# Attention on one core: twelve of 31 head pairs transpose their queries and keys by DMA, and VectorE takes a seventh group of exponentials

## The chip, the cores and the metric

One core of one Trainium2 chip. The metric is device microseconds of that core, as the median of several executions. The profiled span is about 1.8 us shorter than the time of the same execution, so spans are compared only with spans.

Short names: SP is the sync engine, on whose instruction queue nearly all transfers are issued one after the other; PE is TensorE, ACT is ScalarE, DVE is VectorE, POOL is GpSimd. A *pair* is two heads of one batch, a *group* is two score blocks of 128 x 512 that one exponential takes. A pair has four groups.

## The reference

```python
# q, k, v: (8, 8, 512, 64) float32
scale = 1.0 / np.sqrt(q.shape[-1])
scores = np.einsum('bhqd,bhkd->bhqk', q, k) * scale
scores = scores - scores.max(axis=-1, keepdims=True)
attn = np.exp(scores)
attn = attn / attn.sum(axis=-1, keepdims=True)
return np.einsum('bhqk,bhkd->bhqd', attn, v).astype(np.float32)
```

## The kernel before

It walks through 32 pairs. For each: load q, k and v (256 KB each); cast q and k on POOL to fp16 with the two heads side by side (`qkp`); transpose them, eight 128 x 128 transposes on PE into PSUM and one DVE copy back (`tqk`); scores on PE; exponentials on ACT; values on PE with a column of ones for the sum; normalise on DVE; store from SP. Six of the groups have their exponential computed on DVE, in seven passes each. A planner (`Plan`) models the engines with constants in nanoseconds and fixes the order of the instructions.

```python
class Plan:
    SLOT, EXP, EXP_DONE, EXP_FIXED = 216, 853, 1085, 51
    COPY, NORM, NORM_COLUMN = 700, 380, 67
    RAISE, PASSES, LATE = 1216, (867, 822, 1400, 1400, 1400, 1372), 700
    # ... cut
    def for_dve(self, m):                    # may group m go to DVE?
        g = self.groups[m][0][0]
        return (m > 5 and g < self.pairs - 3 and not self.passes
                and not any(x[1] == "raise" for x in self.ready))

    def scores(self, t):
        # ... cut: every fourth group is preceded by a "feed" of its pair
        if m % 4 == 0 and grp[0][0] > 0 and len(grp) == 2:
            self.note(t, "feed", grp[0][0])
# ... cut
    lpool = ctx.enter_context(tc.tile_pool(name="load", bufs=6))
    qpool = ctx.enter_context(tc.tile_pool(name="qk16", bufs=3))
    tpool = ctx.enter_context(tc.tile_pool(name="tqk", bufs=4))

    def feed(g):
        load(g + 5, "kqv")                   # three loads on SP
        cast_qk(g + 3)                       # POOL
        cast_v(g + 2)                        # POOL

    def transposes(g, n, bank):              # half a pair: four on PE
        # ... cut
        for i in range(NI):
            nc.tensor.transpose(tps[g][:, n, i, :], qkp[g][:, n, i, :], ident)

    def copy(g):                             # DVE, PSUM to SBUF
        # ... cut
        nc.vector.tensor_copy(
            out=tqk[g][:, :, :], in_=tps.pop(g).rearrange("p n i c -> p n (i c)"))

    def normalise(u, n):
        # ... cut: reciprocal and multiply on DVE
        while heads and heads[0][2] + NI <= u + n:
            g, h, u0 = heads.pop(0)
            nc.sync.dma_start(               # one store of 128 KB per head, on SP
                out=source(out, g)[:, h], in_=ring[:, u0 % NU : u0 % NU + NI, :])
```

The softmax here doesn't subtract the row's maximum and nothing guards it: scores larger than these inputs give would overflow.

## Time and profile before

| | before |
|---|---|
| time, median of 4 runs | 123.3 us (123.15 to 123.48) |
| profiled span | 121.7 us |
| first exponential begins, last one ends | 5.21 and 117.83 us |
| time lost by ACT between them, added up from the trace | 0.58 us |
| from the last exponential to the end | 3.92 us |
| SP between 20 and 100 us: issuing, waiting | 58.8 us, 13.3 us |

The row for SP is added up from the trace: the durations of its issues, and the pauses of over 0.15 us between them. The exponentials run without a gap and end every 0.918 us; everything else follows them. *Lost* time of ACT means here, and in all that follows, the sum of what the steps from one exponential's end to the next exceed 0.918 us. The time in which no exponential runs at all is less (0.34 us here), because after a pause one takes its full length of some 1.05 us from start to end. Two more lines of before are needed. First from its list of waits (who waited for whom: us in total, times, longest):

```profile
POOL qkp L331 <- DMA k<-in_k_dram: 18.1, 16, 2.9
```

Then the issue of a set of loads in the timeline of SP (start, length, engine, line, operation). Most issues take 0.4 to 0.5 us:

```profile
41.28 0.47 SPq L318 DMA_DIRECT2D k<-in_k_dram  x1
41.79 0.47 SPq L318 DMA_DIRECT2D q<-in_q_dram  x1
42.35 0.42 SPq L318 DMA_DIRECT2D v<-in_v_dram  x1
```

### The profile page before, as it was taken

How to read it: one execution, taken by the hardware profiler on the slowest of the kernel's cores; microseconds unless marked ns; L12 is line 12 of the kernel's file. 1: busy time of each engine (PE TensorE's matmuls, PEld its weight loads, DVE VectorE, ACT ScalarE, POOL GpSimd, SP SyncE). 2: the span in 40 equal slices, each digit the busy share in tenths (PEclk: the TensorE clock that was granted, in tenths of full speed). 3: DMA queues.
4: the chain of work that ended last, by engine and by line, in shares of the span. 5: the costliest groups of instructions: out<-in, count | busy, mean ns of one | idle time of the engine just before them, and what ended most of it. 6: DMA issues, size and time to landing. Idle time of an engine off the chain costs nothing.

```text
span 121.7 us, 3951 instructions
## 1 busy us (share of the span) xinstructions
PE 108.1 (89%) x1557; PEld 67.6 (56%) x1557; DVE 98.5 (81%) x171; ACT 114.4 (94%) x127; POOL 73.9 (61%) x101
## 2 busy tenths in 40 slices
PE   7979788889899798998998998889999998999970
PEld 2556455547466465664565564556655655556550
DVE  1456899989989898699999998986979899876451
ACT  4599999999999999999999999999999999999970
POOL 2368969998487977396587577366794377300000
PEclk9999999999999999999999999999999999999995
DMA  3899999999999989998899967899979995113234
GB/s 117 273 363 384 385 376 384 387 275 282 370 374 352 311 284 318 335 347 276 238 312 297 318 226 251 268 348 343 325 239 281 348 330 196 64 52 126 93 110 152
DMA packets 35603, 33.82 MB, mean 278 GB/s; under 512 B 2688, under 2 KB 35584, under 8 KB 35584
## 3 DMA queue, kind: packets, MB, share of 16 engines
q1 hardware_dynamic: 35152, 33.24, 83.1%
q10 hardware_dynamic: 432, 0.33, 0.9%
q8 instruction: 12, 0.20, 0.7%
q14 instruction: 7, 0.06, 0.2%
HBM read 25.17 MB, written 8.39 MB: 276 GB/s over the span
## 4 chain that ended last, share of the span: by engine, by line
ACT 54%; PE 22%; issue 19%; DVE 2%; ACTq 0%
ACT pt L379 54%; PE st L374 8%; PE o L462 6%; PE st_0a L510 3%; PE tp L348 2%; PE st L553 1%; DVE tqk L353 1%; PE o_last L477 1%; DVE ring L441 1%; PE tp_qb L548 0%; DVE qt L590 0%; DVE obl L490 0%; PE tp_qa L548 0%; PE st_0a L553 0%; DVE rc L440 0%
## 5 line engine op out<-in xcount | busy, mean ns | idle before, releaser
L379 ACT ACTIVATE pt<-st 128x1024 f16<-128x1024 f32 (+1 forms) x120 | 109.4, 1327 | 0.1
L374 PE MATMUL st<-tqk 64*128 64x512 f16 x248 | 48.1, 384 | 7.4 <-ACT pt L379 6.5
L462 PE MATMUL o<-vp,pt 128*128 128x65 f16 x1008 | 46.9, 195 | 1.7 <-ACT pt L379 1.3
L462 PEld LDWEIGHTS <-pt 128*128 128x128 f16 x1008 | 37.0, 98 | 18.8 <-issue 15.0
L331 POOL CAST qkp<-k 128x512 f16<-128x512 f32 x31 | 25.3, 815 | 24.2 <-DMA k<-in_k_dram 18.1
L323 POOL CAST vp<-v 128x512 f16<-128x512 f32 x32 | 27.4, 859 | 1.0 <-DMA v<-in_v_dram 0.9
L374 PEld LDWEIGHTS <-tqk 64*128 64x128 f16 x248 | 13.3, 93 | 20.7 <-issue 12.7
L331 POOL CAST qkp<-q 128x512 f16<-128x512 f32 x30 | 22.7, 756 | 2.4 <-DMA q<-in_q_dram 2.3
L441 DVE TENSOR_TENSOR ring<-o,rc 128x448 f32<-128x448 f32 (+2 forms) x37 | 22.6, 611 | 1.3
L355 DVE COPY tqk<-tp 128x1024 f16<-128x1024 f16 x30 | 20.5, 685 | 3.1 <-PE tp L348 2.8
L348 PE MATMUL tp<-ident,qkp 128*128 128x128 f16 x248 | 19.5, 220 | 0.0
L348 PEld LDWEIGHTS <-qkp 128*128 128x128 f16 x248 | 14.0, 98 | 6.9 <-issue 4.7
L428 DVE SCALAR_TENSOR_TENSOR y<-y,m 128x1024 f32<-128x1024 f32 x12 | 15.9, 1321 | 0.0
L440 DVE RECIPROCAL rc<-o 128x7 f32<-128x7 f32 (+2 forms) x37 | 7.3, 198 | 9.3 <-PE o L462 9.1
L393 DVE TENSOR_SCALAR z<-st 128x1024 uint32<-128x1024 f32 x6 | 7.3, 1221 | 1.1 <-PE st L374 1.1
L428 DVE SCALAR_TENSOR_TENSOR y<-m 128x1024 f32<-128x1024 f32 x6 | 8.2, 1361 | 0.0
L428 DVE SCALAR_TENSOR_TENSOR pt<-y,e 128x1024 f16<-128x1024 f32 x6 | 7.7, 1279 | 0.0
L417 DVE TENSOR_SCALAR e<-z 128x1024 uint32<-128x1024 uint32 x6 | 6.1, 1024 | 0.0
L406 DVE TENSOR_SCALAR m<-z 128x1024 uint32<-128x1024 uint32 x6 | 4.6, 765 | 0.0
L510 PE MATMUL st_0a<-const-bfloat16-1.0 128*128 128x512 bf16 (+1 forms) x11 | 3.5, 482 | 0.8 <-PEq L644 0.8
L510 PEld LDWEIGHTS <-const-bfloat16-1.0 128*128 128x128 bf16 x15 | 1.9, 143 | 2.4 <-issue 2.4
L526 ACT ACT_TABLE_LOAD x1 | 1.3, 1283 | 1.7 <-PEq L644 1.7
(43 smaller groups left out, 18.6 us busy)
## 6 DMA issues: line engine op xcount, KB each, us to landing
out_dram<-ring SPq DMA_DIRECT2D x63, 128.0 KB, 3.8
k<-in_k_dram SPq DMA_DIRECT2D x31, 256.0 KB, 4.8
q<-in_q_dram SPq DMA_DIRECT2D x31, 256.0 KB, 4.9
v<-in_v_dram SPq DMA_DIRECT2D x27, 256.0 KB, 5.3
v<-in_v_dram SPq DMA_DIRECT2D x10, 128.0 KB, 4.4
k<-in_k_dram ACTq DMA_DIRECT2D x2, 128.0 KB, 2.9
q<-in_q_dram SPq DMA_DIRECT2D x2, 128.0 KB, 2.6
out_dram<-obl SPq DMA_DIRECT2D x1, 64.0 KB, 1.8
```

Of the source, the lines that this page charges most:

```text
L323: nc.gpsimd.tensor_copy(out=vps[g % NV][:, :, :, 0:D], in_=raw[g]["v"][:, :, :, :])
L331: eng.tensor_copy(out=t[:, n].rearrange("p i (h d) -> p h i d", h=2), in_=raw[g][name][:, :, :, :],)
L348: nc.tensor.transpose(tps[g][:, n, i, :], qkp[g][:, n, i, :], ident)
L355: nc.vector.tensor_copy(out=tqk[g][:, :, :], in_=tps.pop(g).rearrange("p n i c -> p n (i c)"))
L374: nc.tensor.matmul(st[:, x, :], kc, qc, start=True, stop=True)
L379: nc.scalar.activation(out=pt[:, 0:size, :], in_=st[:, 0:size, :], func=EXP, scale=scale)
L393: nc.vector.tensor_scalar(out=r["z"][:, :, :], in0=r["st"][:, :, :], scalar1=scale * 1.4426950408889634 * 2.0**23, scalar2=(127 + SHIFT) * ...
L428: nc.vector.scalar_tensor_tensor(out=r["pt"][:, :, :] if n == 3 else r["y"][:, :, :], in0=mant if n == 0 else r["y"][:, :, :], scalar=QUAR ...
L440: nc.vector.reciprocal(out=rc[:, 0:n], in_=o[:, x : x + n, D : D + 1])
L441: nc.vector.tensor_tensor(out=ring[:, u % NU : u % NU + n, :], in0=o[:, x : x + n, 0:D], in1=rc[:, 0:n].broadcast_to([P, n, D]), op=AluOp. ...
L462: nc.tensor.matmul(os[u // 7][:, u % 7, :], blocks[(g, c, h)][:, y * P : (y + 1) * P], vps[g % NV][:, h, c, :], start=(c == 0), stop=(c == ...
L510: nc.tensor.matmul(dst[:, 0:n], ones[:, 0:P], ones[:, 0:n], start=True, stop=True)
```

## The change

The intent: exponentials on ACT set the time, and DVE can compute one more group instead if it is spared other work. So pairs 6, 8, ..., 28 get their transposed q and k through a DMA transpose from SBUF to SBUF. That saves 12 copies on DVE and 96 transposes on PE. (v is also loaded in halves for one pair instead of five, `HALVED`: four issues fewer on SP.) It is issued on SP for the pair two ahead, in front of the loads for five pairs ahead. The model's constants are new, the rule for DVE groups allows a seventh, and the last pair does head 0 first, then head 1.

```diff
-    SLOT, EXP, EXP_DONE, EXP_FIXED = 216, 853, 1085, 51
+    SLOT, EXP, EXP_DONE, EXP_FIXED = 216, 853, 181, 64
 ...  (further constants of the model)
+    BY_DMA = (6, 8, 10, 12, 14, 16, 18, 20, 22, 24, 26, 28)
+    LAST_PAIRS, AHEAD, MARGIN, SLACK, MOST = 2, 1, 1.05, 800, 7
-        self.tq = {0: 5800}
+        self.tq = {0: 5800, **{g: 0 for g in self.BY_DMA}}
 ...
-            and g < self.pairs - 3
-            and not self.passes
+            and g < self.pairs - self.LAST_PAIRS
+            and len(self.passes) <= self.AHEAD
+            and len(self.on_dve) < self.MOST
 ...  (order of the last pair; bookkeeping of DVE's model)
+        while self.part_t == 0 and self.next_t in self.BY_DMA:
+            self.next_t += 1
 ...
-    tpool = ctx.enter_context(tc.tile_pool(name="tqk", bufs=4))
+    tpool = ctx.enter_context(tc.tile_pool(name="tqk", bufs=5))
-    HALVED = range(20, 25)
+    HALVED = range(20, 21)
 ...
+    def transpose_by_dma(g):
+        if g not in Plan.BY_DMA:
+            return
+        tqk[g] = tpool.tile([P, 2, S], FP16, tag="tqk", name=f"tqk_{g}")
+        nc.sync.dma_start_transpose(
+            out=tqk[g].rearrange("p n (i c) -> p (n i) c", c=P),
+            in_=qkp[g].rearrange("p n i c -> p (n i c)"),
+        )
     def feed(g):
+        transpose_by_dma(g + 2)
         load(g + 5, "kqv")
```

More of the change, by code (lines that the diff above doesn't have):

```diff
@@ L34 @@
     TO_ACT, TO_DVE, TO_PE = 275, 210, 60
-    COPY, NORM, NORM_COLUMN = 700, 380, 67
-    RAISE, PASSES, LATE = 1216, (867, 822, 1400, 1400, 1400, 1372), 700
-    HURRY = 1200
+    COPY, NORM, RAISE = (615, 700), (307, 390), (1145, 1225)
+    NORM_COLUMN, PASS_DONE = 67, 80
+    PASSES = (690, 950, 1335, 1335, 1335, 1250)
+    FIRST_EXP = 5260
     STEP = 5
     FIRST_UNIT = 4
+    BY_DMA = (6, 8, 10, 12, 14, 16, 18, 20, 22, 24, 26, 28)
+    LATE_NORM, LATE_COPY, HURRY, SOON, BACKLOG = 600, 800, 1400, 220, 1600
+    LAST_PAIRS, AHEAD, MARGIN, SLACK, MOST = 2, 1, 1.05, 800, 7
     def __init__(self, groups, pairs, first):
         self.groups, self.pairs = groups, pairs
-        self.pe, self.act, self.dve = 6000, 4800 + first * 904, 5800
+        self.pe, self.act, self.dve = 7000, self.FIRST_EXP, 7000
         self.m, self.tiled = first, True
@@ L47, in __init__ @@
         for m in range(first):
-            self.exps[m] = 4800 + m * 904 + self.EXP_DONE
+            self.act += self.EXP + self.EXP_FIXED
+            self.exps[m] = self.act + self.EXP_DONE
             self.read.append(self.exps[m])
-        self.tq = {0: 5800}
+        self.tq = {0: 5800, **{g: 0 for g in self.BY_DMA}}
         self.next_t = 1
@@ L59, in __init__ @@
         self.passes = []
+        self.on_dve = []
         self.steps = []
@@ L96, in scores @@
         if on_dve:
+            self.on_dve.append(m)
             self.ready.append((t + self.TO_DVE, "raise", (m,)))
@@ L101, in scores @@
             self.act = begin + self.EXP * len(grp) // 2 + self.EXP_FIXED
-            self.exps[m] = self.act + self.EXP_DONE - self.EXP - self.EXP_FIXED
+            self.exps[m] = self.act + self.EXP_DONE
             self.read.append(self.exps[m])
@@ L175, in step_pe @@
             return self.scores(t)
-        if not one and backlog < 1300 and self.free() < t + 150:
+        if not one and backlog < self.BACKLOG and self.free() < t + self.SOON:
             return
@@ L197, in step_dve @@
             if kind == "norm":
-                self.dve = t + self.NORM + self.NORM_COLUMN * what[1]
-                self.banks[what[2]] = self.dve + self.TO_PE
+                more = self.NORM_COLUMN * what[1]
+                self.dve = t + self.NORM[0] + more
+                self.banks[what[2]] = t + self.NORM[1] + more + self.TO_PE
             elif kind == "copy":
-                self.dve = t + self.COPY
-                self.banks[what[1]] = self.tq[what[0]] = self.dve + self.TO_PE
-            else:
-                self.dve = t + self.RAISE
-                self.read[what[0]] = self.dve + self.TO_PE
+                self.dve = t + self.COPY[0]
+                self.banks[what[1]] = self.tq[what[0]] = t + self.COPY[1] + self.TO_PE
+            else:
+                self.dve = t + self.RAISE[0]
+                self.read[what[0]] = t + self.RAISE[1] + self.TO_PE
                 self.passes += [(what[0], s) for s in range(len(self.PASSES))]
@@ L208, in step_dve @@
             m, s = self.passes[0]
-            if min((x[0] for x in self.ready), default=1e9) > t + self.PASSES[s] - self.LATE:
+            end = t + int(self.MARGIN * self.PASSES[s])
+            late = {"copy": self.LATE_COPY, "norm": self.LATE_NORM, "raise": self.LATE_NORM}
+            if all(x[0] > end - late[x[1]] for x in self.ready):
                 self.passes.pop(0)
                 self.note(t, "pass", m, s)
-                self.dve = t + self.PASSES[s]
+                self.dve = end
                 if s == len(self.PASSES) - 1:
-                    self.exps[m] = self.dve + self.TO_PE
+                    self.exps[m] = end + self.PASS_DONE + self.TO_PE + self.SLACK
     def run(self):
@@ L250 @@
     for g in range(NP):
-        if g == 0:
+        if g in (0, LAST):
             stream += [(g, c, h) for h in range(2) for c in range(NI)]
-        elif g == LAST:
-            stream += [(g, c, h) for c in range(2) for h in range(2)]
-            stream += [(g, c, h) for h in range(2) for c in range(2, NI)]
         else:
```

## The prediction

> **What bounds the kernel now.** I read the page's group list first, then the busy time by stretches, the waits, the DMA issues, and last the tail in the timeline. Busy time by stretches of the span (columns: length, then busy us and count for PE, PEld, DVE, ACT, POOL; clock, DMA share, GB/s):
>
> ```profile
> 10.00:40.00 30.00, 26.94 (x389) 16.64 (x386) 27.68 (x41) 30.00 (x34) 25.65 (x34) 1.00 1.06 356
> 40.00:70.00 30.00, 27.56 (x410) 17.49 (x408) 27.25 (x42) 30.00 (x34) 21.60 (x28) 1.00 0.94 303
> 70.00:100.00 30.00, 27.82 (x424) 17.62 (x421) 26.47 (x43) 30.00 (x35) 19.15 (x25) 1.00 0.92 295
> 100.00:117.80 17.80, 16.72 (x273) 10.87 (x270) 12.57 (x24) 17.80 (x21) 3.29 (x4) 1.00 0.35 115
> ```
>
> ACT is busy for 30.00 of 30.00 us in each stretch. A full busy column alone would not prove a limit, because activations overlap here (mean duration 1.33 us), so I read the ends one by one in the trace: from the 8th ACT instruction (end 9.43 us) to the last full-size one (end 116.85 us) the ends follow each other every 0.91 to 0.92 us, with no longer step except one of 1.09 us near the start. That is 117 steps in 107.42 us, 0.918 us each. ACT is never short of work, and the end of the kernel is its count of exponentials plus a start and a tail. These lines of the groups say the same and give the prices used below:
>
> ```profile
> L379 ACT ACTIVATE pt<-st 128x1024 f16<-128x1024 f32 (+1 forms) x120 | 109.4, 1327 | 0.1
> L374 PE MATMUL st<-tqk 64*128 64x512 f16 x248 | 48.1, 384 | 7.4 <-ACT pt L379 6.5
> ...
> L355 DVE COPY tqk<-tp 128x1024 f16<-128x1024 f16 x30 | 20.5, 685 | 3.1 <-PE tp L348 2.8
> L348 PE MATMUL tp<-ident,qkp 128*128 128x128 f16 x248 | 19.5, 220 | 0.0
> ...
> L428 DVE SCALAR_TENSOR_TENSOR y<-y,m 128x1024 f32<-128x1024 f32 x12 | 15.9, 1321 | 0.0
> ...
> L393 DVE TENSOR_SCALAR z<-st 128x1024 uint32<-128x1024 f32 x6 | 7.3, 1221 | 1.1 <-PE st L374 1.1
> L428 DVE SCALAR_TENSOR_TENSOR y<-m 128x1024 f32<-128x1024 f32 x6 | 8.2, 1361 | 0.0
> L428 DVE SCALAR_TENSOR_TENSOR pt<-y,e 128x1024 f16<-128x1024 f32 x6 | 7.7, 1279 | 0.0
> L417 DVE TENSOR_SCALAR e<-z 128x1024 uint32<-128x1024 uint32 x6 | 6.1, 1024 | 0.0
> L406 DVE TENSOR_SCALAR m<-z 128x1024 uint32<-128x1024 uint32 x6 | 4.6, 765 | 0.0
> ```
>
> The first line: idle 0.1 us before 120 activations. The second: PE's longest wait is for ACT (6.5 us, to free a scores buffer), so PE follows ACT and not the reverse. The chain of waits gives ACT only 54% and calls 19% "issue"; with ACT gapless I take both for the same queue of exponentials. DVE is the helper engine: six groups of scores get their exponential there.
>
> **What the Trainium skill says.** Three pages bear on this. "VectorE: DVE Perf Modes", section The three transpose paths: 128x128 in bf16 takes 390 ns on TensorE and lands in PSUM, 1309 ns through the DMA crossbar and lands in SBUF. The trace has the TensorE path much cheaper than that in a row (248 transposes, union 19.5 us, 79 ns each), and no DMA transpose at all. "Advanced Engine Details and Errata", section X-Bar Transpose (TRN2): such transposes are as fast as regular DMAs, 350 to 400 GB/s; "DMA: Bandwidth & Descriptors", section Latency and other measured facts, has 261 GB/s for a non-contiguous case. No run so far shows either. Ordinary loads here run at 256 KB per 0.66 us when the queue is full (landing to landing), so the low figure would be about 1.0 us for the 256 KB of one pair (estimate from that page). What decides for me is the rate, since eight blocks go in one instruction; but 8 times 1309 ns, 10.5 us, is the bad case and comes back as a rival.
>
> **The change, part by part.**
>
> Off PE: 12 pairs, 8 transposes each, 96 of 248: 96 x 79 ns = 7.5 us of PE, plus changes of tiling. PE is not on the path, so this is worth 0 directly; it gives PE slack to catch up after a late input.
>
> Off DVE: 12 copies of 685 ns, 8.2 us. Onto DVE: a seventh group. One group by the rows above: 1.221 + 0.765 + 1.024 + 1.361 + 2 x 1.321 + 1.279 = 8.29 us. Net +0.07 us on an engine with some 90% busy in the middle. So the copies pay for exactly one more group; this is the sense of the change.
>
> Off ACT: the built order confirms it: ACT has one instruction fewer, DVE five fewer (minus 12, plus 7), PE 192 fewer counting weight loads. One exponential of 0.918 us leaves the engine that sets the end: **-0.92 us**. It is the only gain on the path.
>
> Start: the first pair is built as before, 0. Tail: the last pair's blocks are reordered (head 0 whole, then head 1). In the tail now (timeline) all 16 last matmuls start only when a normalisation has freed their bank:
>
> ```profile
> 117.70 0.67 PE L477 MATMUL o_last<-vp,pt 128*128 128x65 f16 x16 [0.19 <-DVE ring L441]
> ...
> 118.41 0.18 DVE L489 RECIPROCAL rc_last<-o_last 128x4 f32<-128x4 f32 x1 [0.21 <-PE o_last L477]
> 118.62 0.42 DVE L490 TENSOR_TENSOR obl<-o_last,rc_last 128x256 f32<-128x256 f32 x1
> ```
>
> The last exponential ends at 117.83, so at best four matmuls remain after it and about 0.2 us is to be had; the bank and the normalisations before it are still there in the new order, so I book -0.1 us.
>
> Added on the DMA queue: 12 transposes of 256 KB inside SBUF, 3.1 MB beside 33.8 MB. The supply in the middle: per two pairs (8 groups, less the share on DVE, about 7.0 us) six loads of 0.66 us and four stores of 0.34 us, 5.3 us. At an estimated 1.0 us for a transpose this is 6.3 of 7.0, so bandwidth suffices, with little left. The tile pool has one transposed buffer more, and the loads of k land 6 to 13 us before their pair's first scores from pair 5 on, so loads may slip some us unpunished.
>
> Latency of the transpose: it is issued two pairs ahead, on the SP queue just ahead of the loads for five pairs ahead. In the old trace I compare the issue of those loads of k with the first scores two pairs later: gaps for the even pairs from 4 to 26 are 5.3, 5.3, 6.4, 6.1, 8.6, 8.4, 7.0, 7.8, 4.7, 6.7, 6.4, 5.5 us, mean 6.5. What has to fit in: issue (0.4 us for a load), and the landing behind what is already queued:
>
> ```profile
> k<-in_k_dram SPq DMA_DIRECT2D x31, 256.0 KB, 4.8
> ```
>
> That is 4.8 us, of which the own transfer is 0.66. With 1.0 us in its place: about 5.1 + 0.4 = 5.5 us against 6.5. So most fit and three or four are late by up to 0.8 us. Against that PE issues scores some 0.6 to 1.0 us before ACT needs them (three buffers of 0.918 us less the matmuls). The overrun left for ACT I book as **+0.15 us** in all.
>
> Sum: -0.92 - 0.1 + 0.15 = -0.87 us; 123.18 - 0.87 = 122.3 us.
>
> **The rivals.**
>
> (1) Late transposes: the wait of scores on PE for transposed keys, now 0.9 us in all, replaces the gain. For it: the margin above is 1 us, DMA shares are around 1 for two thirds of the span, and the new order treats these pairs as always ready. Against: PE has 7.5 us less to do and can run up to the buffers again; ACT hides up to 0.6 us each. If each of 12 came 1 us later than I think, with 0.5 us of it reaching ACT, the cost is 6 us less catching up: 124 to 128 us.
>
> (2) DMA becomes the bound: if a transpose holds the 16 queues for 2.5 us, two pairs need 7.8 us against 7.0, 0.8 x 12 = 10 us, less some 5 us of slack in the loads: +5 us, 127 us. At 10.5 us each it would be far above 200. Against it: the rates of two pages, and that one every second pair looks like a dose chosen for what the queue bears. The SP queue too could be the bound if the issue is long; it waits 17.9 us in all for normalised results today:
>
> ```profile
> SPq L449 <- DVE ring L441: 17.9, 15, 2.6
> ```
>
> so it has room for about 1.5 us per transpose.
>
> (3) DVE late: the new order lets the next group begin while one pass of the last is left. If normalisations are held up, PE waits for banks. But the load is the same (+0.07 us) and the two banks serve 12 transposes fewer. Cost at most some tenths: 122.5.
>
> (4) All of it hidden and the tail better than booked: 121.9.
>
> **Range and chances.** The gain has a hard ceiling: one exponential and 0.2 us of tail, 1.12 us, so 122.06, and run scatter is about 0.15; 2% faster would be under 120.7, and nothing in the change reaches it: 3%. Rivals 1 and 2 are the only way to over 125.6; I give them 10%, since the seventh group and the new constants look fitted to one another. Most of the rest lies at 122.0 to 123; a mild form of rival 1 stretches the upper end. Range 121.8 to 124.0.
>
> **What would show it right or wrong.** Right: 119 activations in the second loop, still at 0.918 us from end to end with idle near 0.1 us; DVE copies x18 and seven of each pass; ACT's last end near 116.9 us; DMA transposes landing within about 6 us of issue; PE's wait for ACT larger than 6.5 us. The DMA step is wrong if steps between ACT's ends exceed 0.95 us at the even pairs from 6 on, with scores waiting for a DMA on the transposed tile; the SP step is wrong if its issue takes over 1.5 us; the tail step is wrong if the last exponential to the end is still 3.9 us or more. The prediction as a whole is wrong if ACT gains gaps of over 1.5 us in sum, or if the transpose occupies the queue for over 2 us.

## The result and the profile after

| | before | after |
|---|---|---|
| time, median of 4 runs | 123.3 us (123.15 to 123.48) | 129.42 us (129.27 to 129.79) |
| profiled span | 121.7 us | 127.6 us |
| first exponential begins, last one ends | 5.21 and 117.83 us | 4.71 and 123.47 us |
| time lost by ACT between them | 0.58 us | 7.64 us |
| from the last exponential to the end | 3.92 us | 4.13 us |
| SP between 20 and 100 us: issuing, waiting | 58.8 us, 13.3 us | 67.9 us, 4.3 us |
| one step of two pairs in the middle | 6.93 us | 7.55 us |

The ratio is 1.050, with a 95% interval of 1.0472 to 1.0529: slower. Here and below, a ratio is the mean time of one kernel's runs over that of the other's runs of the same rounds, so it is not quite the ratio of the medians quoted. Executions over 1.5% slower than the fastest of the same kernel are left out of the means. The last row is the time from the first scores of pair 6 to the first scores of pair 28, divided by 11.

The spans differ by 5.86 us. From the trace this is: start 0.50 earlier, one exponential less 0.92, lost time of ACT 7.06 more, tail 0.21 more. So **all of the loss is lost time of ACT**. The chain that ended last, by engine, was ACT 54%, PE 22% and "issue" 19% before. Of after it reads:

```profile
DMA 52%; PE 10%; DVE 9%; SPq 9%; POOL 8%; issue 5%; ACT 4%; POOLq 0%
```

The groups of after (busy us and mean ns, then the idle time just before and its main releaser):

```profile
L401 ACT ACTIVATE pt<-st 128x1024 f16<-128x1024 f32 (+1 forms) x119 | 109.9, 1075 | 6.1 <-PE st L396 5.9
L396 PE MATMUL st<-tqk 64*128 64x512 f16 x248 | 48.6, 397 | 17.4 <-DMA tqk<-qkp 13.1
...
L377 DVE COPY tqk<-tp 128x1024 f16<-128x1024 f16 x18 | 12.3, 683 | 3.0 <-PE tp L370 3.0
```

The reader is to see three things: 119 exponentials and 18 copies, as intended; ACT waits 5.9 us for scores; and scores wait 13.1 us for the DMA transpose. The waits of after add who else waits, POOL for the loads of k, 31.0 us against 18.1:

```profile
POOL qkp L343 <- DMA k<-in_k_dram: 31.0, 21, 3.3
PE st L396 <- DMA tqk<-qkp: 13.1, 9, 2.1
```

By stretches (same columns as in the prediction: length; busy us and count of PE, PEld, DVE, ACT, POOL; clock, DMA share, GB/s), ACT now has 26.21 us in the middle stretch where it had 30.00, and the DMA share (the time that the packets took, as a share of 16 engines' time; it can pass 1) stands at 1.14 throughout, where it fell to 0.92:

```profile
10.00:40.00 30.00, 23.77 (x328) 14.14 (x325) 28.96 (x38) 29.44 (x32) 24.36 (x31) 1.00 1.14 327
40.00:70.00 30.00, 25.21 (x347) 14.93 (x348) 23.27 (x35) 26.21 (x29) 17.61 (x24) 0.89 1.14 315
70.00:100.00 30.00, 23.88 (x356) 14.60 (x354) 28.12 (x39) 29.07 (x33) 19.73 (x25) 1.00 1.14 321
```

The view of the transposed tile gives the issue (ns, least, median, most) and the landing, counted from the start of the issue:

```profile
L353 SPq DMA_TRANSPOSE tqk<-qkp x12: 1237/1271/2134, 19.9 to 102.1; - x12
...
DMA to landing us min/median/max: 4.0/4.9/6.6
```

The landing is what the prediction said. The issue is three times what it took for granted. SP's timeline shows how it sits ahead of the loads:

```profile
42.49 1.25 SPq L353 DMA_TRANSPOSE tqk<-qkp  x1
43.79 0.57 SPq L330 DMA_DIRECT2D k<-in_k_dram  x1
```

In nine of the twelve pairs the first scores start 0.05 us after the transpose has landed: they wait for it and for nothing else. In the other three they start 1.1 us after it. The transposes are late because SP is late with them: the prediction had measured, in before, that SP issues the loads of k at this place 0.44 us (mean) after the first scores of the current pair. In after the transpose at this place goes out 2.17 us after them; with 5.02 us (mean) to the landing that is 7.2 us, and ACT gets through two pairs in 6.93.

**A second cost: half clock.** PE's timeline (in brackets the idle time before, and what ended it) and the stretches around it show a wait of 1.98 us, after which the matmuls of one shape go from 0.39 to 0.61 us and the granted clock falls to 0.60 in the stretch after it:

```profile
40.30 0.39 PE L396 MATMUL st<-tqk 64*128 64x512 f16 x2 [1.98 <-DMA tqk<-qkp]
...
40.99 0.61 PE L396 MATMUL st<-tqk 64*128 64x512 f16 x2
```

```profile
42.00:45.00 3.00, 3.00 (x45) 2.00 (x43) 1.60 (x5) 2.04 (x3) 2.06 (x5) 0.60 1.09 382
45.00:48.00 3.00, 3.00 (x55) 1.87 (x52) 2.93 (x5) 3.00 (x4) 0.46 (x1) 1.00 1.18 299
```

In the records the clock stands at half from 41.01 to 44.43 us and once more from 64.91 to 68.32. In those stretches PE is busy without a break while ACT is not fed. Adding up ACT's 7.64 us of lost time by place: 4.75 at the first groups of DMA pairs, 2.18 at the third and fourth groups of pairs 10 and 16 (the two stretches at half clock), 0.50 at the start, 0.2 elsewhere. The second stretch at half clock followed a wait of 2.09 us. But a third wait of this kind, 2.06 us up to 72.55, was followed by none, and in `e1_unread` (below) half clock began after a wait of 1.07 us; so what sets it off is not shown.

### The profile page after: what moved, and what is told of

Read it like the earlier page. It is cut to its first block, busy times and chain, and to the rows that moved or that the text cites.

```text
span 127.6 us, 3742 instructions
## 1 busy us (share of the span) xinstructions
PE 103.3 (81%) x1461; PEld 62.3 (49%) x1461; DVE 99.8 (78%) x166; ACT 114.8 (90%) x126; POOL 72.7 (57%) x101
## 4 chain that ended last, share of the span: by engine, by line
DMA 52%; PE 10%; DVE 9%; SPq 9%; POOL 8%; issue 5%; ACT 4%; POOLq 0%
DMA k<-in_k_dram 28%; DMA tqk<-qkp 13%; DMA v<-in_v_dram 9%; POOL qkp L343 6%; PE o L484 5%; PE st L396 4%; ACT pt L401 4%; SPq L353 3%; SPq L330 3%; DMA out_dram<-ring 3%; DVE ring L463 3%; SPq L471 2%; POOL vp L335 2%; DVE y L450 1%; DVE pt L450 1%
## 5 line engine op out<-in xcount | busy, mean ns | idle before, releaser
L396 PE MATMUL st<-tqk 64*128 64x512 f16 x248 | 48.6, 397 | 17.4 <-DMA tqk<-qkp 13.1
L484 PE MATMUL o<-vp,pt 128*128 128x65 f16 x1008 | 49.6, 197 | 1.5 <-ACT pt L401 0.7
L484 PEld LDWEIGHTS <-pt 128*128 128x128 f16 x1008 | 38.6, 99 | 23.9 <-issue 21.1
L343 POOL CAST qkp<-k 128x512 f16<-128x512 f32 x31 | 23.5, 759 | 33.1 <-DMA k<-in_k_dram 31.0
L450 DVE SCALAR_TENSOR_TENSOR y<-y,m 128x1024 f32<-128x1024 f32 x14 | 18.9, 1350 | 0.0
L377 DVE COPY tqk<-tp 128x1024 f16<-128x1024 f16 x18 | 12.3, 683 | 3.0 <-PE tp L370 3.0
L370 PE MATMUL tp<-ident,qkp 128*128 128x128 f16 x152 | 12.6, 220 | 0.3 <-DVE rc L462 0.2
L370 PEld LDWEIGHTS <-qkp 128*128 128x128 f16 x152 | 8.6, 98 | 5.8 <-issue 4.2
L450 DVE SCALAR_TENSOR_TENSOR y<-m 128x1024 f32<-128x1024 f32 x7 | 10.1, 1447 | 0.0
L450 DVE SCALAR_TENSOR_TENSOR pt<-y,e 128x1024 f16<-128x1024 f32 x7 | 9.3, 1324 | 0.0
L428 DVE TENSOR_SCALAR m<-z 128x1024 uint32<-128x1024 uint32 x7 | 6.6, 947 | 0.0
```

The lines of the kernel that those rows point to most:

```text
L343: eng.tensor_copy(out=t[:, n].rearrange("p i (h d) -> p h i d", h=2), in_=raw[g][name][:, :, :, :],)
L377: nc.vector.tensor_copy(out=tqk[g][:, :, :], in_=tps.pop(g).rearrange("p n i c -> p n (i c)"))
L396: nc.tensor.matmul(st[:, x, :], kc, qc, start=True, stop=True)
L428: nc.vector.tensor_scalar(out=r["m"][:, :, :], in0=r["z"][:, :, :], scalar1=0x007FFFFF, scalar2=0x3F800000, op0=AluOp.bitwise_and, op1=Alu ...
L450: nc.vector.scalar_tensor_tensor(out=r["pt"][:, :, :] if n == 3 else r["y"][:, :, :], in0=mant if n == 0 else r["y"][:, :, :], scalar=QUAR ...
L484: nc.tensor.matmul(os[u // 7][:, u % 7, :], blocks[(g, c, h)][:, y * P : (y + 1) * P], vps[g % NV][:, h, c, :], start=(c == 0), stop=(c == ...
```

## The experiments

They ask, in this order: what does it cost to *wait* for the transpose, what does its *presence* cost with nobody waiting, and which property of it (issue, bytes, order) does that. In many of them the result is wrong; that is said each time. "Correct" means it agrees with the reference.

### 1. Taking the wait away, taking the transpose away, and issuing it earlier

In `e1_unread` the transpose is issued as before but into a tile that nobody reads; the scores use the transposed tile of the pair before (wrong). `e2_none` also leaves the transpose out (wrong). `e3_early` is correct.

```diff
# e1_unread
-        tqk[g] = tpool.tile([P, 2, S], FP16, tag="tqk", name=f"tqk_{g}")
+        tqk[g] = tqk[g - 1] if g - 1 in tqk else None
+        unread = tpool.tile([P, 2, S], FP16, tag="tqd", name=f"tqd_{g}", bufs=2)
-            out=tqk[g].rearrange("p n (i c) -> p (n i) c", c=P),
+            out=unread.rearrange("p n (i c) -> p (n i) c", c=P),
+                gt = g - 1 if g in Plan.BY_DMA else g      # scores read tqk[gt]
# e2_none: as e1_unread, but transpose_by_dma issues nothing
# e3_early: half a pair earlier in the order
-        transpose_by_dma(g + 2)                            # in feed
+            if what == "scores" and args[0] % 4 == 1:      # after the scores, in the main loop
+                transpose_by_dma(groups[args[0]][0][0] + 3)
```

> The twelve DMA transposes are issued as in the changed kernel, at the same place in the queue, but into tiles that nothing reads; the scores of these pairs read the transposed tile of the pair before (wrong result on purpose). Only the wait of PE for the transpose is gone; its bandwidth and its issue time stay. Theory A (the transpose comes late because it stands behind a full queue, and PE's wait for it is the whole loss): about 122.3 us, ACT without gaps. Theory B (the DMA queue has too little bandwidth, the loads come late with or without the wait): 126 us or more, with PE or POOL waiting for loads and ACT gaps. Theory C (the new order or the seventh group costs the time): stays near 129.4.

> As the run before, and the transposes are not issued at all (wrong result on purpose). Theories A and B: 122.2 us, which is what the seventh group on VectorE is worth with all inputs in time (one exponential of 0.918 us less on ACT). Theory C: over 123.3, since the order is the same.

> Correct kernel: each transpose is issued half a pair earlier (after the second group of the pair three ahead, in place of the start of the pair two ahead), some 1.8 us. Theory A: most of the waits, 0.05 to 1 us at ACT each, vanish: 122.3 to 123.5 us. Theory B: nothing gained over the whole, 127 to 129.5 us. Theory C: 129.4.

| run | time, median (range, runs) | ratio to before, 95% | time lost by ACT in the profiled run |
|---|---|---|---|
| after | 129.42 (129.27 to 129.79, 4) | 1.050, 1.0472 to 1.0529 | 7.64 us |
| e1_unread | 127.42 (126.22 to 127.61, 4) | 1.0316, 1.0255 to 1.0377 | 3.88 us |
| e2_none | 123.23 (122.73 to 124.03, 4) | 1.0003, 0.9948 to 1.0058 | 0.65 us |
| e3_early | 130.94 (129.56 to 132.6, 4) | 1.0585, 1.0505 to 1.0665 | 8.59 us |

The wait for the transpose is worth 1.8 percentage points of 5.0 (give or take 0.7, an estimate from the two intervals). The other 3.1 points come from its mere presence: nobody waits for it in `e1_unread`, and yet ACT goes short. Its waits show where it goes instead; POOL waits for k, and PE's transposes of the other pairs wait for POOL:

```profile
POOL qkp L343 <- DMA k<-in_k_dram: 22.2, 16, 3.4
PEld L371 <- POOL qkp L343: 7.2, 13, 1.5
```

Of the 3.88 us that ACT loses in this profiled run, 2.4 lie in or just after stretches at half clock (10.2 us of them before the tail), so the two costs are mixed here. Half clock does not carry the 3.1 points by itself: the two runs with more of the clock granted (0.986 and 0.982) took 127.48 and 127.61 us, the profiled one (0.958) 126.22.

Without the transposes ACT is gapless again in each stretch, here the last (ACT 30.00), in spite of all the rest of the change:

```profile
70.00:100.00 30.00, 26.04 (x384) 15.96 (x384) 27.96 (x40) 30.00 (x34) 24.87 (x28) 1.00 0.97 311
```

So the order, the constants and the seventh group cause no loss. Nor is there a gain that the runs show: `e2_none` is what the change would be with free transposes, and it equals the kernel before within 0.7 us either way. More on that under 5.

`e3_early` cannot be read as "earlier doesn't help" alone: the issue did not come earlier. The transposes around 34 and 58 us went out at 34.62 and 58.42 us, in after at 34.71 and 57.48. Moving it forward in the order of a queue that runs late moves nothing.

### 2. Bytes, or the kind of transfer?

`e4_fewer_loads` takes 12 of the v loads out (wrong); `e5_unread_fewer` does so in `e1_unread`. `e6_unread_copy` has a plain copy of the same 256 KB in place of each unread transpose, `e12_three_small` three plain copies of 8 KB each (all wrong).

```diff
# e4_fewer_loads (on after), e5_unread_fewer (on e1_unread)
+    NO_V = range(7, 31, 2)
+            if name == "v" and g in NO_V:
+                continue                                   # cast_v reads v of the pair before
# e6_unread_copy, on e1_unread
-        nc.sync.dma_start_transpose(
-            out=unread.rearrange("p n (i c) -> p (n i) c", c=P),
+        nc.sync.dma_start(
+            out=unread.rearrange("p n s -> p (n s)"),
# e12_three_small, on e1_unread, in place of the transpose
+        for n in range(3):
+            x = slice(32 * n, 32 * n + 32)
+            nc.sync.dma_start(out=unread[:, 0, x], in_=qkp[g][:, 0, 0, x])
```

> The changed kernel without the loads of v for the twelve odd pairs from 7 to 29 (their values are taken from the pair before, wrong result on purpose): 3.1 MB less on the queue, as much as the transposes added. Theory A: the queue ahead of a transpose is one load (0.65 us) shorter in every two pairs, so the waits shrink but not all vanish: 123 to 127 us. Theory B: the bandwidth is back to that of the kernel before, 122.3 us. Theory C: 129.4.

> Both at once: the transposes are issued but unread (as in e1_unread) and the twelve loads of v are left out (as in e4_fewer_loads); wrong result on purpose. Theory B2 (the queue was all but full before the change: by the landings it needed some 6.6 us of the 6.9 us that ACT takes for two pairs, so 1.0 us more per two pairs does not fit, and the wait for a transpose adds to it): with the load taken off and the wait gone nothing is left, 122.7 to 123.5 us, as without any transposes. Theory S (the 1.24 to 2 us of issuing a transpose on the SP queue, in series with all other issues, is the loss, not the bandwidth): the twelve issues are still there, so 125 us or more. Theory A (waiting alone): cannot be, after e1_unread.

> As e1_unread, but in place of each transpose an ordinary copy of the same 256 KB inside SBUF, into a tile that nothing reads (wrong result on purpose). Its issue should take 0.45 us and its landing 0.65 us after the one before it, like a load, against 1.24 and 1.0 us. Theory B2: about two thirds of the extra queue time stay, so 124 to 126 us, between 123.2 and 127.4. Theory S or a theory that the crossbar as such disturbs the queue: 123.2 to 123.6, as without transposes.

> As e1_unread, but each transpose is replaced by three plain copies of 128x32 fp16 (8 KB each) into a tile that nothing reads (wrong result on purpose): as much issue time on SP as a transpose (3 x 0.45 us against 1.24), next to no bytes. Theory S: 126 to 128 us, like e1_unread. Theory B2: 123.2 to 124 us, like e2_none.

| run | time, median (range, runs) | ratio to before, 95% |
|---|---|---|
| e4_fewer_loads | 125.39 (124.84 to 128.07, 5) | 1.0149, 1.0085 to 1.0214 |
| e5_unread_fewer | 123.55 (122.92 to 123.83, 4) | 1.002, 0.9976 to 1.0064 |
| e6_unread_copy | 123.45 (123.3 to 123.98, 4) | 1.0026, 0.9987 to 1.0066 |
| e12_three_small | 132.21 (129.85 to 134.08, 4) | none |

The profiled run of `e4_fewer_loads` was slow, so only its ratio is used: with 12 loads less, 3.5 of the 5.0 points are gone though the scores still wait for their transposes. `e12_three_small` scatters so much that the rule leaves one fast run, 129.85 us; it has no ratio. Its fastest run is above all of `e1_unread`.

A plain copy of the same bytes at the same place costs nothing that can be told from zero, where theory B2 had expected 124 to 126 us. So it is **not the bytes as such**, but what the transpose does with them. SP's timeline of `e6_unread_copy`: the copy's issue takes 0.47 us, where the transpose took 1.25.

```profile
41.27 0.47 SPq L354 DMA_DIRECT2D tqd<-qkp  x1
41.79 0.60 SPq L330 DMA_DIRECT2D k<-in_k_dram  x1
```

And the steps from one landing to the next while the queue is full are 0.63 us for the copy, 0.65 for a load, 0.35 for a store, and 1.0 for the transpose (medians, from the trace). The transpose is dearer in both ways, on SP and in the queue, and 12 loads less pay for it (`e5_unread_fewer`).

`e12_three_small` was to add issues with hardly a byte. From SP's timeline, three copies of 8 KB, the longest of the twelve sets:

```profile
43.60 3.15 SPq L356 DMA_DIRECT2D tqd<-qkp  x3
46.80 0.59 SPq L330 DMA_DIRECT2D k<-in_k_dram  x1
```

The other eleven sets took 1.76 to 2.31 us, the median is 1.8; the transpose takes 1.39 us in `e1_unread` (mean). So the stand-in is somewhat longer on SP than the transpose, and in the queue it is about half as long: the small copies land 0.18 us apart. By expectation this was for theory S (126 to 128 us) and against B2 (123.2 to 124). ACT went short in it (27.89 of 30) although the DMA share, 0.85, was below the 0.99 that `e6_unread_copy` has in this stretch:

```profile
70.00:100.00 30.00, 24.56 (x337) 14.35 (x334) 26.29 (x36) 27.89 (x30) 19.46 (x22) 0.93 0.85 254
```

The likeliest reading is that time on SP by itself can do as much harm as the transposes do. That the small pieces (64 bytes) disturb the queue in some other way is not excluded, and with one fast run and a profile of a slow one the size stays uncertain.

### 3. Relieving SP

If the length of the issue is the cause, other issues taken off SP must bring the time back. `e10_pool_loads` issues 12 loads of v from POOL (correct), `e9_unread_pool_loads` does that in `e1_unread`. `e13_merged_stores` joins the two stores of a pair where the ring buffer allows it, 25 issues fewer (correct); `e15_unread_merged` in `e1_unread`; `e17_unread_merged_pool` has both reliefs in `e1_unread`. `e18_before_merged` is the control: joined stores in the kernel before (correct). The unread ones are wrong.

```diff
# e9, e10, e17
+    BY_POOL = range(7, 31, 2)
-            nc.sync.dma_start(out=t[:, :, :, :], in_=source(src, g))
+            queue = nc.gpsimd if name == "v" and g in BY_POOL else nc.sync
+            queue.dma_start(out=t[:, :, :, :], in_=source(src, g))
# e13, e14, e15, e17, e18: hold the store of head 0 until head 1 is normalised
+            both = h == 0 and g < LAST and u0 % NU + 2 * NI <= NU
+            if both and len(heads) < 2:
+                break
+            if both and heads[1][:2] == (g, 1):
+                if heads[1][2] + NI > u + n:
+                    break
+                del heads[:2]
+                nc.sync.dma_start(out=source(out, g), in_=ring[...])   # 256 KB, cut
+                continue
```

> As e1_unread (transposes issued, unread, wrong result on purpose), but the loads of v of the twelve odd pairs from 7 to 29 are issued from the POOL queue instead of the SP queue: same bytes on the same 16 engines, some 0.5 us less of issue on SP for each. From the traces SP is 94% occupied with issuing between 20 and 100 us in e1_unread (69.6 us of issue and 0.06 us between two), so it may be SP that is full. Theory S (serial issue on SP is the limit): close to e5_unread_fewer, 123 to 124.5 us. Theory B2 (queue bandwidth is the limit): stays at 126.5 to 128 us. If POOL, which casts, loses more by issuing than it has to spare, casts come late and the run says nothing for S.

> Correct kernel: the changed kernel with the same twelve loads of v issued from the POOL queue. Theory S: SP reaches each transpose earlier, so it lands before its scores: 122.5 to 125 us. Theory B2: 128 to 130 us.

> Correct kernel: the changed kernel, with the two output stores of a pair joined into one of 256 KB where the ring allows it: 25 issues fewer on SP (0.41 us and 0.06 us of gap each, 11.8 us in all, against 12 transposes at 1.24 us), same bytes, all transposes kept. Theory S (serial issue on SP): most of the loss goes, 123 to 126 us. If the bytes or the time of the transposes on the engines were the loss: 128.5 to 130 us.

> As e1_unread (127.4 us: transposes issued, unread, wrong result on purpose), with the stores joined as in e13_merged_stores. Theory S: the loss against e2_none (123.2 us) all but goes, 123 to 124.5 us. If it is the transposes' time on the queue: 126.5 to 127.5 us.

> As e1_unread (ratio to the kernel before 1.0316), with the stores joined as in e15_unread_merged (1.0148) and twelve loads of v issued from POOL as in e9_unread_pool_loads (1.0159); wrong result on purpose. Theory S, serial issue alone: the two reliefs add up, 1.000 to 1.005, as without any transposes. If something else of the transposes (their time on the queue, the casts on POOL) holds the second half: 1.010 to 1.016.

> Correct kernel: the kernel before with the stores joined. Theory S: SP waits 13 us between 20 and 100 us there and ACT has no gap, so fewer issues change nothing, 0.995 to 1.005. If joining is a gain of its own: 0.985 to 0.99, and then e13_merged_stores and e15_unread_merged say less for S.

| run | time, median (range, runs) | ratio to before, 95% |
|---|---|---|
| e10_pool_loads | 128.45 (127.48 to 129.36) | 1.0416, 1.0347 to 1.0485 |
| e13_merged_stores | 127.99 (127.08 to 129.87, 6) | 1.0366, 1.0328 to 1.0404 |
| e9_unread_pool_loads | 126.24 (125.06 to 127.89; fast 125.06 and 125.46) | 1.0159, 1.0105 to 1.0213 |
| e15_unread_merged | 125.38 (124.22 to 125.68, 4) | 1.0148, 1.0102 to 1.0194 |
| e17_unread_merged_pool | 126.15 (124.51 to 132.94, 6) | 1.0191, 1.0137 to 1.0244 |
| e18_before_merged | 123.62 (123.05 to 123.98, 6) | 1.0027, 0.9994 to 1.006 |

Each relief brings about half of the loss of the unread kernel back, which neither theory had expected; in the kernels that read the transpose only 0.8 and 1.3 of 5.0 points. There the transposes went out sooner, 1.40 us (`e10_pool_loads`) and 1.18 us (`e13_merged_stores`) after the first scores instead of 2.17, but took 5.54 and 5.84 us to land instead of 5.02 (means, the stretched issue included), so little was won. The control shows that joining stores gains nothing of itself.

All this spoke for SP's issues in part. `e17_unread_merged_pool`, with 37 issues fewer, should by theory S have been near 1.00 and was at 1.0191, but it is not a clean test. In the three runs that issue loads from POOL some passes on DVE take 2.1 to 3.0 us (one each in `e9` and `e10`, three in `e17`), where none takes over 1.66 us in before, after, `e1`, `e2` or `e15`. In `e17` PE then waits for a normalisation behind such a pass:

```profile
30.11 2.54 DVE L454 SCALAR_TENSOR_TENSOR y<-m 128x1024 f32<-128x1024 f32 x1
33.48 0.30 PE L501 MATMUL o<-vp,pt 128*128 128x65 f16 x4 [1.30 <-DVE ring L467]
```

Soon after it ACT loses 1.27 us in one step, of 3.31 us in that run. So `e17` does not show that theory S is wrong.

What speaks against its plain form is that SP never gets free. Between 20 and 100 us it issues for 67.9 us in after, 69.6 in `e1_unread`, 70.0 in `e15_unread_merged` and 70.2 in `e17_unread_merged_pool`; where issues were removed, the transpose's own issue stretched, from a mean of 1.40 us in after to 1.77 and 1.97 in these two. So an issue of a transpose seems to be in part a wait for something beyond SP.

### 4. What the stream of transfers can deliver

This reading was formed after the runs, from their traces; no run was made to test it. For every pair I took the time by which the load of q lands ahead of the pair's first scores, its *lead*, in the profiled run of each kernel. The step of two pairs is that of the table above. If the lead shrinks, transfers come more slowly than ACT consumes, though ACT may not be short yet; the pace of the loads is then the step plus the lead lost per step (nine steps lie between the middles of the two columns).

| run | transposes in it | step of two pairs, us | lead, pairs 8 to 11 | lead, pairs 26 to 29 | pace of the loads, us |
|---|---|---|---|---|---|
| before | none | 6.93 | 10.1 | 10.8 | 6.86 |
| e2_none | none | 6.94 | 10.2 | 12.0 | 6.74 |
| e6_unread_copy | plain copies | 6.98 | 9.2 | 8.3 | 7.08 |
| e5_unread_fewer | unread, 12 loads less | 6.95 | 9.0 | 8.6 | 6.99 |
| e15_unread_merged | unread | 7.02 | 8.8 | 5.7 | 7.36 |
| e17_unread_merged_pool | unread | 7.15 | 10.4 | 8.1 | 7.41 |
| e1_unread | unread | 7.37 | 7.4 | 6.5 | 7.47 |
| e9_unread_pool_loads | unread | 7.27 | 8.7 | 5.3 | 7.65 |
| e13_merged_stores | read | 7.32 | 10.0 | 10.4 | 7.28 |
| after | read | 7.55 | 10.3 | 10.5 | 7.53 |

(Where the lead does not fall, the pace may be that of the buffers coming free, and the stream could do better. That holds for the first rows, and for after and `e13_merged_stores` too: there the scores wait, and the loads follow.) With all loads and unread transposes in it, **the stream takes 7.4 to 7.65 us for two pairs, also with SP relieved, and ACT needs 6.93**. With plain copies it takes 7.1.

The size fits what the queue has to do. From the steps between landings, two pairs are 6 x 0.65 + 4 x 0.35 = 5.3 us without a transpose, 5.9 with a plain copy, 6.3 with a transpose. But the queue is not filled with such steps alone: between 20 and 95 us, even in the runs that pressed it hardest (after, `e6_unread_copy`, `e15_unread_merged`), 16 to 17% of the time is left over when the bytes are priced at these steps. A part of that is seen singly: about every 10 us an instruction fetch of 16 KB takes one DMA engine some 0.95 us, and the next load lands 0.8 us later than due in before, 1.3 in after. Divided by 0.835, the three sums are 6.3, 7.1 and 7.5 us (estimates). The last two lie at the paces measured with copies and with unread transposes. That is no independent check, since the 0.835 is taken from three of these runs; what it says is that one and the same share is left over with copies and with transposes. And it fails for `e12_three_small`: 5.8 us of the queue, like the plain copy, yet its profiled run (a slow one) has a pace of 8.2 us.

SP's own time is a rival of the same size: at the mean lengths in after, six loads of 0.55, four stores of 0.45, a transpose of 1.38 and 0.06 us between two make 7.1 us for two pairs, and the same sum with the lengths of `e12_three_small` 7.8 (estimates).

This also tells why the forms differ so much at one pace. Loads are issued five pairs ahead and have some 10 us of lead to lose first: `e15_unread_merged` lost 3.1 us of it, and ACT was busy all the time in the last two stretches, here the third:

```profile
70.00:100.00 30.00, 26.27 (x394) 16.14 (x391) 27.17 (x41) 30.00 (x34) 19.39 (x24) 1.00 1.14 322
```

A transpose that is read has no such lead. It rides in the same stream, two pairs ahead, and as soon as the stream runs late, the scores wait for it: in after the loads keep their lead, 10.5 us, and the whole lag, 11 x (7.55 - 6.93) = 6.8 us, falls on ACT. That is nearly the 7.06 us of its added lost time.

**What stays open:** whether SP's long issue (1.24 us and more) or the transfer itself (1.0 us against 0.63) sets the pace. The stretched issues and the longer landings under 3 speak for the transfer, the reliefs and `e12_three_small` for a share of SP; with a transpose the two can't be had apart.

### 5. The dose, the seventh group and the end

`e7_every_fourth` has six DMA pairs (correct), `e8_no_dma_pairs` none and so all copies on DVE. `e11_none_old_end` and `e16_none_old_end_fixed` are `e2_none` with the last pair's old order (wrong), `e14_merged_old_end` is `e13_merged_stores` with it (correct).

```diff
# e7_every_fourth
-    BY_DMA = (6, 8, 10, 12, 14, 16, 18, 20, 22, 24, 26, 28)
+    BY_DMA = (6, 10, 14, 18, 22, 26)
# e8_no_dma_pairs
+    BY_DMA = ()
# e11, e14, e16: the last pair's blocks as in the kernel before
+            stream += [(g, c, h) for c in range(2) for h in range(2)]
+            stream += [(g, c, h) for h in range(2) for c in range(2, NI)]
# e14, e16 only: the last head is not begun while others are left
+                if (g, h) == (self.pairs - 1, 1) and len(self.todo) > 1:
+                    continue
```

> Correct kernel: only pairs 6, 10, 14, 18, 22 and 26 go by DMA (the planned order still puts seven groups on VectorE). Theory B2: four pairs need 13.2 + 1.0 = 14.2 us of queue against 13.9 on ACT, an excess of 0.3 us six times, which the loads' lead covers: 123 to 124.5 us. Theory A2 (each transpose is late on its own because it stands behind some seven transfers, whatever the total): half the loss of the changed kernel stays, 126 to 126.5 us.

> Correct kernel: no pair goes by DMA, all transposes on TensorE and all copies on VectorE, with the new constants; the order it makes still has seven groups on VectorE. If VectorE can carry seven groups beside all 31 copies (98.5 + 8.3 = 106.8 us of work in 121): 122.5 to 123.3 us, and the transposes by DMA bought nothing. If VectorE then comes late with normalisations and copies: 124 us or more, and the copies did have to go.

> As e2_none (no transposes, wrong result on purpose), with the last pair's blocks in the order of the kernel before. It tells what the new order of the last pair costs: from the last exponential to the end the kernel before took 3.92 us, e2_none 4.59. If the order of the last pair is the cause, the tail is back to 3.9 and the time 122.3 to 122.7 us; if the tail is longer because ACT ends earlier while TensorE and VectorE do not, it stays at 4.4 or more and 123.2 us.

> Correct kernel: as e13_merged_stores, and the last pair's blocks in the order of the kernel before, with the plan held from starting the last head before all others. If theory S holds and the new order of the last pair costs 0.6 us: 0.6 us under e13_merged_stores, 122.3 to 125.5 us; at 122.3 it would beat the kernel before.

> As e2_none (no transposes, wrong result on purpose), with the last pair's blocks in the old order and the last head held back until all others are begun. If the order of the last pair made the tail longer: tail 3.9 to 4.1 us and 122.3 to 122.8 us. If the tail is longer only because ACT ends earlier: 4.4 us or more and 123.2 us.

| run | time, median (range, runs) | ratio to before, 95% |
|---|---|---|
| e7_every_fourth | 127.18 (126.84 to 128.02, 4) | 1.0332, 1.0281 to 1.0383 |
| e8_no_dma_pairs | 123.3 (122.95 to 123.57, 4) | 1.0006, 0.996 to 1.0051 |
| e11_none_old_end | 122.19 (122.0 to 123.91, 7) | 0.9922, 0.9885 to 0.9958 |
| e14_merged_old_end | 128.04 (127.56 to 129.09, 6) | 1.0394, 1.0354 to 1.0435 |
| e16_none_old_end_fixed | 123.67 (122.38 to 124.37, 6) | 1.0001, 0.9953 to 1.0049 |

Two of these are spoiled. `e8_no_dma_pairs` gave NaN: with 31 copies on DVE, the planned order finished the seventh group (in pair 26) only after the last head, and the end of the kernel, which is written for one given last head, no longer held. Its time is not used. What remains of it is that DVE, in the planner's model, does not get a seventh group done in time beside all the copies. `e11_none_old_end` gave NaN for a like reason, the last head began before the one ahead of it; its 0.9922 is therefore not taken as a gain. With that mended, `e16_none_old_end_fixed`, it is 1.0001.

`e7_every_fourth` with half the dose fits neither of its expectations. ACT loses only 2.11 us in it, 1.7 of them at a half clock that began within a wait of 1.34 us for a transpose, but it takes 6.74 us from the last exponential to the end. There an instruction fetch at 120.81 us held one DMA engine just as the last stores were under way; they took 4 us instead of 1.8. From its DMA view between 119 and 124 us (us to landing last):

```profile
q8 instruction: 1, 0.02, 1.2%
...
out_dram<-ring SPq DMA_DIRECT2D x3, 128.0 KB, 4.1
```

That is seen in one profiled run, so how much of the 3.3% comes from it in the other runs is not known.

**Where the gain of the seventh group went.** In `e2_none` the stretch from the first exponential to the end of the last is 111.78 us, in before 112.62: the 0.84 us are there. The tail took 0.67 of them back, 4.59 us against 3.92 (one profiled run each). Its timeline at the end (last exponential at 116.75 us) shows the last matmuls waiting for a normalisation on DVE:

```profile
117.03 0.65 PE L500 MATMUL o_last<-vp,pt 128*128 128x65 f16 x16 [0.75 <-DVE rc L463]
117.72 0.18 DVE L512 RECIPROCAL rc_last<-o_last 128x4 f32<-128x4 f32 x1 [0.29 <-PE o_last L500]
```

They start 0.28 us after the last exponential; in before 0.13 us ahead of it, and the reciprocal that follows comes 0.97 us after it instead of 0.58. With the old order of the last pair (`e16_none_old_end_fixed`) the tail is 4.52 us, so it isn't the order; nor is `e14_merged_old_end` faster than `e13_merged_stores`. Whether the later groups on DVE push the last normalisations back was not tested.

No version beat the kernel before.

## Why the prediction was wrong

It said 122.3 us, 121.8 to 124.0; it is 129.42. Two of its steps failed, the supply and the latency of the transpose. By its own steps:

- **The supply term failed: "At an estimated 1.0 us for a transpose this is 6.3 of 7.0, so bandwidth suffices, with little left."** The 1.0 us was right (262 GB/s from landing to landing, and "DMA: Bandwidth & Descriptors" of the Trainium skill, section Latency and other measured facts, had 261 for a non-contiguous case). The slip was to price the queue at its clean steps, and the issue on SP like that of a load. The stream took 7.4 to 7.65 us for two pairs with unread transposes in it; whether the transfer or the issue on SP is the cause stays open. The trace of before had a warning in it: between 20 and 60 us its 12.71 MB, priced at 0.65 us for 256 KB, fill 31.5 of 40 us, although seven transfers were in flight on average.
- **The latency term failed by what it rested on.** "About 5.1 + 0.4 = 5.5 us against 6.5." Issue to landing was 5.02 us (mean), as said (the landing is counted from the start of the issue, so the 0.4 was counted twice; it changed nothing). The 6.5 us was the gap in the old trace, and SP kept that date no longer: 2.17 us after the scores instead of 0.44. So not "three or four" came late but nine, and +0.15 us became 7 us. The prediction had named ACT gaps of over 1.5 us in sum as what would prove it wrong; they are 7.64.
- **The issue was taken for 0.4 us.** It was 1.24 to 2.13 us. In rival 2 the text had argued from SP's 17.9 us of waiting that it "has room for about 1.5 us per transpose". SP's waits between 20 and 100 us did fall, from 13.3 to 4.3 us, and the room was still not there: a wait in a queue that works in order sits at a fixed place, and what comes behind it is late all the same (this reason is argued, no run tests it).
- **Rival 1 came, with rival 2 behind it.** "Late transposes" named the symptom and was given 124 to 128 us; rival 2 named the stream and was given 127. Together they had 10%. `e1_unread` splits them: 1.8 points for the wait, 3.1 for the transposes' presence.
- **Not foreseen: half clock.** Two of three waits of about 2 us were followed by 3.41 us at half clock, and 2.18 us of ACT's lost time lies there. No term of the sum had this.
- **The -0.92 us was right on ACT and wrong for the end.** 119 exponentials, 0.84 us less in `e2_none`. The tail, booked at -0.1 us, was +0.21 in after and +0.67 in `e2_none`. So with free transposes the change shows no gain (0.7 us either way), where 0.87 us was forecast.
- **Right:** 18 copies and seven of each pass on DVE; the eight blocks of a pair at 1.0 us instead of 8 x 1309 ns; landing within 6.6 us; no loss from the new order and constants (`e2_none`, 1.0003). Two readings were slightly off without effect: 96 x 79 ns is 7.6 us, and the loads of k land up to 14.4 us ahead, not 13.

## What to carry to other kernels

Before a transfer is added to a queue that is always full, take its real pace from the trace (bytes over a long stretch, where the queue is what limits), not the sum of clean steps, and ask for the length of the issue as well as of the transfer. A gap read from the old trace holds only if the engine that issues keeps its dates; waits in an in-order queue are not room. And what an unbroken engine saves must be followed to the last store: here the tail took most of it back.

## What the Trainium skill lacked or had wrong

- "DMA: Bandwidth & Descriptors", section Issuing engines are not separate DMA queues, calls the time on the sequencer to initiate a DMA "usually small relative to the DMA itself". Here a transpose of 256 KB took 1.24 to 2.13 us to issue on SP (up to 3.43 in `e17_unread_merged_pool`) against 1.0 us of the queue; a plain copy 0.47 against 0.63; a copy of 8 KB in small pieces 0.60 against 0.18 (medians).
- "Advanced Engine Details and Errata", section X-Bar Transpose (TRN2), has transposes as fast as regular DMAs, 350 to 400 GB/s. Here 256 KB took 1.0 us (262 GB/s) where a plain copy at the same place took 0.63 (416 GB/s).
- "TensorE: Matmul & The Clock Gate", section Why this matters for your kernels, warns of idle gaps of PE above some 3 us. Here half clock for 3.41 us followed waits of 1.98 and 2.09 us (not one of 2.06), and in `e1_unread` one of 1.07.
- "Runtime: NRT & Kernel Launch", section Instruction fetch mechanics, calls the cost of crossing a 16 KiB block of instructions mostly hidden. For the engine that may be so; but each such fetch takes one DMA engine some 0.95 us. They come about every 10 us here, the next load lands 0.8 to 1.3 us late, and in one profiled run the last stores came 2 us late.
